# Attention in one Trainium2 core: written orders for VectorE and ScalarE, finer steps, other places of loads and another handover

## The chip, the cores and the metric

The kernel runs on one core of a Trainium2 chip. It has five engines that each work through their own list of instructions in order: TensorE (PE; its weight loads are listed apart as PEld), VectorE (DVE), ScalarE (ACT), GpSimd (POOL) and SyncE (SP), which here only issues DMAs. Sixteen DMA engines move the data. The metric is the device time of one execution in microseconds, as the median of the runs; a difference of 0.3% (4.4 us) is about what a measurement of this kernel can tell from no change.

## The reference, cut to what matters

One encoder layer over 1024 frames of width 1024, in float32:

```
h  = RMSNorm(x);  P = h @ W_in            # q, k, v of 8 + 8 heads of 64, forget values, gates
A  = causal softmax(q k^T / 8 + c[t] - c[s]) v        # 8 "fox" heads; c = running sum of log f
B  = softmax(q k^T / 8 + rel_bias[clip(t - s)]) v     # 8 "band" heads; own and 8 earlier chunks of 64
y  = sigmoid(gA) * (A @ Wa) + sigmoid(gB) * (B @ Wb)
x  = x + y @ W_out
x  = x + relu(RMSNorm(x) @ W_up)^2 @ W_down;  final RMSNorm
```

Every softmax is exact: the row's largest value is taken off before the exponential, and the sum divides the result at the end.

## The kernel before, in words

Every large product runs as three matmuls on values that are split in a high and a low part (`wh`, `wl` of a weight, `xh`, `xl` of an operand), and the projections use Strassen's seven products. The program has these stages: projections of q, k, v and gates (to about 412 us of the profile), **attention** (to about 687 us), the second branch product, whose tiles are called `m` (to 740 us), the output projection `o` (to 844 us), and the feed-forward part. Only attention and the branch product are touched by the change.

**A head of attention.** The 16 heads are worked through in the order of `HEADS`: heads 0 to 7 are fox heads (causal, widths of 128 to 1024 keys), heads 8 to 15 are band heads (at most 640 keys). A head has eight query blocks of 128 rows. For each block, *S* (`score`) makes the scores on PE in a PSUM tile `s`; the pool `pss` holds two of them. Then DVE adds the mask (`wide`) or the bias tile (`bc`) in place and takes the row's smallest value into `mn` (line 498, profiled as CUSTOM_DVE_ANT_0 with a short READ_ACCUMULATOR behind it; scores are negated, so the smallest is the largest). Then ACT takes the exponential into the probabilities `p` (line 509), and the `s` tile is free again. Then, for a group of up to four 128x128 blocks, *T* (`turn`) transposes `p` on PE into a PSUM tile `pt`, ACT rounds it to the high part `th` (line 829) and DVE takes the low part `tl` (line 830). *P* (`weigh`) multiplies `th` and `tl` with the values and sums in the one PSUM tile `pv`, which ACT copies to `both` (line 790). In the string of a head, the scores are those of the head after it.

**What sets the order.** On PE the order is written out: `FOX_TURN` and `BAND_TURN` are strings of letters S, T, P and F that are worked through once for each head, and everything on PE is issued through an object that keeps the program's order. `INTRO` brings a few letters forward. The DMAs on SP keep the program's order as well. On DVE, ACT and POOL the order is left to the scheduler, which places instructions by its own estimate of time; what comes out is a fixed list too, since each engine works through its list in order.

**Filling.** From head 9 on, the letter F puts three matmuls of the first branch product (`m_c_h_1`, 128 columns of gate and 512 frames each) between the attention's matmuls. Its weight `wrab` is loaded one block ahead (`fetch` in `fill`), rounded on ACT (line 718) and its low part made on POOL (line 720); the gate `z` is loaded too, and the result goes to `m_dram`.

**Loads of a head.** At the end of a head's scores, `load_head` issues `qk` and `sk` of the head after next and `load_bias` its bias tile (one DMA of 128x640, a negation on POOL on line 458, and two memsets that block the corners). After the second group of an odd head, `reciprocals` turns the sums of the exponentials into factors, writes them to `r_dram` in four DMAs and reads them back spread over partitions (`rb`, two DMAs) at once; POOL multiplies with them (line 811).

**Handover.** After the last head, the band heads' results are read back from `o_dram` (`olt`) and split for the branch product; then for each of 16 tiles the gate, the earlier part `m` and the product are put together, and split on POOL (lines 875 to 886).

Of the kernel before, what the change touches and what calls it, by code (L numbers as in the profile page):

```python
# [40 lines left out]
INTRO = "TTPTTTPP"  # L41
FOX_TURN = "TTTSPSTTPSPTTSPPTSTPTSPSPPPS"
BAND_TURN = "TSTFSFFTFPSTSTFPPSTFTSPPTSFFPSPP"
# [47 lines left out]
def hybrid_block(ctx: ExitStack, tc: tile.TileContext, xT, xN, g1, wall, wf, fb, relb, g2, g3, outT):  # L91
# [359 lines left out]
    def load_bias(n, eng):  # L451

        pr, hh = HEADS[n]
        if pr >= 4:
            return
        bc = biases[n] = aps.tile([P, BAND], F32, tag=f"bc{n % 2}", name=f"bc{n}")
        eng.dma_start(bc, relb[2 * pr + hh])
        G.tensor_scalar(bc, bc, -1.0, None, op0=ALU.mult)
        G.memset(bc[0:64, BAND - 64:BAND], BIG)
        G.memset(bc[64:128, 0:64], BIG)  # L460

    def load_head(n, eng):
# [4 lines left out]
        if n < 2:  # L467
            sks.append(p.tile([SK, 2, S], F32R, tag="sk", name=f"sk{n}"))
            G.memset(sks[n][HD:SK].bitcast(F32), 0.0)
            G.memset(sks[n][HD:HD + 3, 1, :].bitcast(F32), 1.0)  # L470
# [11 lines left out]
    def score(n, i, bank, te, ve):  # L482
# [5 lines left out]
        if i == 0:  # L488
            smalls[n] = aps.tile([P, 8], F32, tag=f"mn{n % 2}", name=f"mn{n}")
        spans = [(max(off, HALF * x), min(off + W, HALF * (x + 1))) for x in range(2 if off + W > HALF else 1)]  # L490
        rows = slice(i * P, (i + 1) * P)
        for t, w in enumerate((qk, sk)):
            for a, b in spans:
                keys = slice(j0 * P + a - off, j0 * P + b - off)
                te.matmul(bank[:, a:b], w[:, 1, rows], w[:, 0, keys], start=t == 0, stop=t == 1)
        x = bank[:, off:off + W]
        more = wide[:, S - W:S] if pr >= 4 else biases[n][:, BAND - W:BAND]
        ve.tensor_tensor_reduce(x, x, more, 1.0, 3.0e38, ALU.add, ALU.min, smalls[n][:, i:i + 1])  # L498

    def soften(n, i, bank):  # L500
# [7 lines left out]
        with tc.issue_after(sigmoids[-1]):  # L508
            A.activation(p[:, :W], bank[:, off:off + W], AF.Exp, scale=-1.0, bias=smalls[n][:, i:i + 1],  # L509
# [64 lines left out]
    def project_qk(pr):  # L574
        def out(row, h, src):
            t = etile("qk")
            V.scalar_tensor_tensor(t, src, -0.125 if row == 0 else 1.0, rstd[:, hs(h)], op0=ALU.mult, op1=ALU.mult)
# [53 lines left out]
    G.affine_select(out=wide[:, S - P:S], in_=wide[:, S - P:S], compare_op=ALU.is_ge, fill=BIG, base=0, pattern=[[-1, P]],  # L631
# [15 lines left out]
    sent = 0  # L647

    def send(te=TO):
        nonlocal sent  # L650
        if sent == len(chunks):
            return
        n, i = chunks[sent]
        bank = pss.tile([P, S], F32, tag="s", name="s")
        score(n, i, bank, te, V)
        soften(n, i, bank)
        sent += 1
        if i == 7 and n + 2 < 16:
            load_head(n + 2, LO)
            load_bias(n + 2, LO)  # L660

    for n, ins in enumerate(chain(steps, last)):
# [3 lines left out]
        with tc.issue_after(ins):  # L666
            for _ in range(AHEAD[n]):
                send()
# [7 lines left out]
    ol = opool.tile([P, 4, S], F32R, tag="ol", name="ol")  # L676
    apq.append(pool(astack, "apq1", "right"))
# [552 lines left out]
```

## Time and profile before

| | |
|---|---|
| median of 3 runs | 1457.67 us (1457.08 to 1460.63) |
| the profiled execution | 1460.32 us, of which 1458.6 us are the span of the instructions |
| PE, DVE, ACT, POOL busy | 96%, 59%, 48%, 59% of the span |
| mean granted TensorE clock | 0.991 |

A matmul's end is modelled in the profile and matmuls overlap, so a busy PE is not a PE at its best: what counts is how far one start is from the next. The sharpest reading is therefore by stages, in stretches that are cut where each head does the same thing.

### The profile page before, as it was taken

How to read it: one execution, taken by the hardware profiler on the slowest of the kernel's cores; microseconds unless marked ns; L12 is line 12 of the kernel's file. 1: busy time of each engine (PE TensorE's matmuls, PEld its weight loads, DVE VectorE, ACT ScalarE, POOL GpSimd, SP SyncE). 2: the span in 40 equal slices, each digit the busy share in tenths (PEclk: the TensorE clock that was granted, in tenths of full speed). 3: DMA queues.
4: the chain of work that ended last, by engine and by line, in shares of the span. 5: the costliest groups of instructions: out<-in, count | busy, mean ns of one | idle time of the engine just before them, and what ended most of it. 6: DMA issues, size and time to landing. Idle time of an engine off the chain costs nothing.

```text
span 1458.6 us, 20521 instructions
## 1 busy us (share of the span) xinstructions
PE 1402.2 (96%) x6658; PEld 1167.7 (80%) x6658; DVE 860.2 (59%) x1349; ACT 697.8 (48%) x1351; POOL 861.2 (59%) x688
## 2 busy tenths in 40 slices
PE   7999999999999988988999999999999999999997
PEld 5787888888878877877788888888888888888886
DVE  7756445443268865754428864444545568999644
ACT  8534333344358875655336543333333344344654
POOL 1377776778822253323783677777776645557463
PEclk9999999999999999999999999999999999999998
DMA  8546667763457688886756244444444875679263
GB/s 275 151 113 190 184 193 218 207 196 123 142 170 214 179 227 225 253 237 197 257 179 200 89 143 150 145 153 152 153 152 157 284 234 170 168 244 230 88 211 121
DMA packets 138069, 268.94 MB, mean 184 GB/s; under 512 B 19490, under 2 KB 21538, under 8 KB 134890
## 3 DMA queue, kind: packets, MB, share of 16 engines
q1 hardware_dynamic: 90106, 182.50, 41.1%
q10 hardware_dynamic: 44656, 77.26, 16.6%
q0 software_dynamic: 3200, 7.88, 2.4%
q8 instruction: 52, 0.85, 0.2%
q14 instruction: 55, 0.45, 0.1%
HBM read 173.49 MB, written 86.21 MB: 178 GB/s over the span
## 4 chain that ended last, share of the span: by engine, by line
PE 75%; DMA 7%; issue 5%; POOL 4%; DVE 4%; ACT 3%; SPq 0%; POOLq 0%; ACTq 0%; DVEq 0%
PE u L214 39%; PE dS L214 11%; PE dA L214 5%; PE o L214 5%; PE s L104 3%; PE pv L104 3%; PE m L214 3%; PE pt L104 3%; DMA wrab<-wall 2%; POOL wl_A L163 2%; DMA bc<-relb 2%; DMA wr<-wall 2%; PE m L104 1%; ACT p L509 1%; PE u L104 1%
## 5 line engine op out<-in xcount | busy, mean ns | idle before, releaser
L163 POOL TENSOR_TENSOR wl_A<-wr,wh_A 128x512 fp32r<-128x512 f32 x118 | 158.8, 1354 | 90.6 <-ACT wh_A L161 74.8
L163 POOL TENSOR_TENSOR wl_S<-S,wh_S 128x512 fp32r<-128x512 f32 x102 | 136.1, 1338 | 32.7 <-ACT wh_S L161 32.0
L161 ACT CAST wh_S<-S 128x512 fp32r<-128x512 f32 x105 | 64.6, 621 | 113.0 <-PE u L214 44.2
L830 DVE TENSOR_TENSOR tl<-pt,th 128x512 fp32r<-128x512 f32 (+1 forms) x144 | 89.7, 642 | 40.4 <-ACT th L829 39.8
L161 ACT CAST wh_A<-wr 128x512 fp32r<-128x512 f32 x105 | 64.9, 620 | 89.4 <-PE u L214 45.0
L509 ACT ACTIVATE p<-s,mn 128x640 f32<-128x640 f32 (+7 forms) x128 | 90.6, 710 | 34.1 <-DVE mn L498 32.6
L163 POOL TENSOR_TENSOR wl_S<-ks,wh_S 128x512 fp32r<-128x512 f32 x48 | 67.0, 1421 | 53.6 <-ACT wh_S L104 53.6
L567 DVE TENSOR_TENSOR u<-u,u 128x512 f32<-128x512 f32 x70 | 48.8, 697 | 74.4 <-PE u L214 71.7
L829 ACT CAST th<-pt 128x512 fp32r<-128x512 f32 (+1 forms) x144 | 76.6, 555 | 25.6 <-PE pt L104 25.0
L104 PE MATMUL pt<-ident,p 128*128 128x128 f32 x528 | 78.5, 279 | 7.9 <-DVE tl L830 7.7
L184 POOL TENSOR_TENSOR S<-wr,wr 128x512 f32<-128x512 f32 x35 | 46.0, 1314 | 57.4 <-DMA wr<-wall 37.0
L104 PEld LDWEIGHTS pt<-ident,p 128*128 128x128 f32 x528 | 63.6, 143 | 17.2 <-DVE tl L830 6.3
L104 PE MATMUL s<-qk 128*128 128x384 f32 (+2 forms) x192 | 59.6, 365 | 13.7 <-ACT p L509 13.7
L104 PE MATMUL pv<-th,v 128*128 128x512 f32 (+1 forms) x192 | 65.0, 348 | 4.2 <-ACT lo L787 2.1
L163 POOL TENSOR_TENSOR wl_A<-ka,wh_A 128x512 fp32r<-128x512 f32 x32 | 46.0, 1448 | 35.4 <-ACT wh_A L104 35.4
L104 PE MATMUL pv<-tl,v 128*128 128x512 f32 (+1 forms) x192 | 62.4, 344 | 2.2 <-DVE tl L830 2.2
L810 POOL TENSOR_TENSOR on<-on,lo 128x512 f32<-128x512 f32 x16 | 20.5, 1284 | 73.7 <-PE pv L104 40.7
L276 ACT CAST qkh<-qk 128x512 fp32r<-128x512 f32 x32 | 19.9, 621 | 88.3 <-DMA qk_dram<-qkl 34.0
L985 ACT ACTIVATE v<-v 128x512 f32<-128x512 f32 x64 | 40.3, 632 | 44.7 <-DVE v L984 44.7
L560 DVE TENSOR_TENSOR u<-u,c 128x512 f32<-128x512 f32 x35 | 24.5, 699 | 58.6 <-PE u L214 56.6
L498 DVE CUSTOM_DVE_ANT_0 s<-s,wide 128x128 f32<-128x128 f32 (+3 forms) x64 | 48.6, 764 | 14.0 <-PE s L104 13.5
L498 DVE CUSTOM_DVE_ANT_0 s<-s,bc 128x640 f32<-128x640 f32 (+2 forms) x64 | 42.4, 662 | 23.7 <-PE s L104 18.5
(420 smaller groups left out, 4705.2 us busy)
## 6 DMA issues: line engine op xcount, KB each, us to landing
wr<-wall SPq DMA_DIRECT2D x235, 256.0 KB, 3.6
a_dram<-at ACTq DMA_DIRECT2D x64, 256.0 KB, 2.7
xT<-a_dram SPq DMA_DIRECT2D x64, 256.0 KB, 4.7
qk<-qk_dram SPq DMA_DIRECT2D x15, 1024.0 KB, 8.7
qk_dram<-qkh ACTq DMA_DIRECT2D x96, 128.0 KB, 2.5
a_dram<-v ACTq DMA_DIRECT2D x48, 256.0 KB, 2.0
xB<-a_dram SPq DMA_DIRECT2D x44, 256.0 KB, 4.6
z_dram<-zt ACTq DMA_DIRECT2D x32, 256.0 KB, 2.2
```

The lines of the kernel that those rows point to most:

```text
L104: return lambda *a, **kw: tc.keep_in_program_order(getattr(self.eng, name)(*a, **kw))
L161: (act.tensor_copy if act is G else act.copy)(wh, src)
L163: lows.append(eng.tensor_tensor(wl, src, wh.bitcast(F32), op=ALU.subtract))
L184: eng.tensor_tensor(t, raw(3), raw(2), op=ALU.add)
L214: done = eng.matmul(bank, w[wi], x[xi], start=(first and t == 0), stop=(t == n - 1 and not part), skip_group_check=part or not first)
L498: ve.tensor_tensor_reduce(x, x, more, 1.0, 3.0e38, ALU.add, ALU.min, smalls[n][:, i:i + 1])
L509: A.activation(p[:, :W], bank[:, off:off + W], AF.Exp, scale=-1.0, bias=smalls[n][:, i:i + 1], accum_out=smalls["den", pr][:, 8 * hh + i:8 ...
L560: V.tensor_tensor(banks[1], banks[3], c22, op=ALU.add)
L567: V.tensor_tensor(banks[b], banks[b], u2, op=ALU.add)
L829: A.copy(th, pt)
L830: V.tensor_tensor(tl, pt, th.bitcast(F32), op=ALU.subtract)
L985: A.activation(v, v, AF.Square)
```

## The change

All attention steps get letters of their own, and DVE and ACT keep the program's order too: S makes the scores, R takes the smallest (DVE), E the exponential (ACT), T transposes, H rounds (ACT), L takes the low part (DVE), P multiplies, V copies `pv` out (ACT), F fills, M ends a filled tile (DVE), O splits a band head's result for the handover. There are strings for a fox head, a band head and the last head.

The scores are no longer negated: the mask and the bias tile carry minus the large number, and the smallest of the negated sum is taken in the same instruction by its factor of -1. So the bias tile is used as it is loaded: two tiles are kept, their corners are set once, and two DMAs of 64x576 fill the rest; the negation and the memsets of each head are gone. The bias is loaded when the smallest value of the last block has been taken, no longer with the scores. `rb` is read back when the head's `pv` has been copied out, no longer right after the write. Weights and gates for filling are fetched four tiles ahead instead of one, and their rounding stands in ACT's order.

At the end, the last head's results stay on the chip (`o3h`, `o3l`, made by DVE and ACT), the other band heads' results are read back and split while the last head runs (O), and the branch product begins with four tiles whose last quarter waits for the last head (`begun`). Its tiles come in another order, and the split behind it moves from POOL to DVE.

```diff
-INTRO = "TTPTTTPP"
-FOX_TURN = "TTTSPSTTPSPTTSPPTSTPTSPSPPPS"
-BAND_TURN = "TSTFSFFTFPSTSTFPPSTFTSPPTSFFPSPP"
+INTRO = "THLPTHLTTHPHLL"
+FOX_HEAD = "THSSRRETTSLPHEHTLSRTLPHERPHTSLTELSHVTPHRLRELTHSEPTSHLRPEPPLPHRLEPV"
+BAND_HEAD = "FFTSFHTHFRLSLRMPETSHETPLFRHETSPLRHFVSTPEHLTRHPLLSFETFPRHLESPPSMRRVEE"
+LAST_HEAD = "THLTHLFFFFMTHPPFLFFFMTPTHFLHFTFFPVLTMHPFHLTHFFFLPLOOOPOOMOPV"
...
     def load_bias(n, eng):
...
-        bc = biases[n] = aps.tile([P, BAND], F32, tag=f"bc{n % 2}", name=f"bc{n}")
-        eng.dma_start(bc, relb[2 * pr + hh])
-        G.tensor_scalar(bc, bc, -1.0, None, op0=ALU.mult)
-        G.memset(bc[0:64, BAND - 64:BAND], BIG)
-        G.memset(bc[64:128, 0:64], BIG)
+        if n < 10:
+            bands.append(aps.tile([P, BAND], F32, tag=f"bc{n % 2}", name=f"bc{n}"))
+            G.memset(bands[-1][0:64, BAND - 64:BAND], -BIG)
+            G.memset(bands[-1][64:128, 0:64], -BIG)
+        bc = biases[n] = bands[n % 2]
+        eng.dma_start(bc[0:64, 0:BAND - 64], relb[2 * pr + hh, 0:64, 0:BAND - 64])
+        eng.dma_start(bc[64:P, 64:BAND], relb[2 * pr + hh, 64:P, 64:BAND])
...
-        ve.tensor_tensor_reduce(x, x, more, 1.0, 3.0e38, ALU.add, ALU.min, smalls[n][:, i:i + 1])
+        ve.tensor_tensor_reduce(x, x, more, -1.0, 3.0e38, ALU.add, ALU.min, smalls[n][:, i:i + 1])
...
+    def take_lowest(ve=VO):
+        if len(cut) < len(chunks):
+            n, i = chunks[len(cut)]
+            lowest(n, i, made[len(cut)], ve)
+            cut.append(None)
+            if i == 7 and n + 2 < 16:
+                load_bias(n + 2, LO)
...
+        for _ in range(4):
+            fetch()
+        yield
+        halves(0)
         yield
         for n, (c, h) in enumerate(todo):
-            if n + 1 < len(todo):
-                fetch()
+            fetch()
+            if h == 0:
+                halves(c + 1)
...
+    def spread_reciprocals(pr):
         rb = ap0.tile([P, S], F32, tag="rb", name=f"rb{pr}")
...
+        if pr == 3:
+            VO.tensor_tensor(o, o, rb, op=ALU.mult)
+            AO.copy(o3h[:, hs(h)], o)
+            VO.tensor_tensor(o3l[:, hs(h)], o, o3h[:, hs(h)].bitcast(F32), op=ALU.subtract)
+            return
...
+    def round_p():
+        pt, th, tl = turns[0][len(turns[1])]
+        turns[1].append(AO.copy(th, pt))
+
+    def low_p():
+        pt, th, tl = turns[0][len(turns[2])]
+        turns[2].append(VO.tensor_tensor(tl, pt, th.bitcast(F32), op=ALU.subtract))
...
+    for c in range(4):
+        begun[c, 0] = psm[0].tile([P, HALF], F32, tag="d", name=f"m{c}_0_0")
+        branch(begun[c, 0], c, 0, range(3))
+    for c, h in [(c, h) for d in (0, 4) for h in range(2) for c in range(d, d + 4)]:
...
-        split((mop[h][0][:, c, :], mop[h][1][:, c, :]), m, G)
+        split((mop[h][0][:, c, :], mop[h][1][:, c, :]), m, V)
```

How the lists of the engines change at three places follows. In a row, `out<-in` are the program's names, with a number for each buffer.

**PE, end of one fox head and start of the next, before.** The row `s_4878` holds the last and widest scores (1024 keys) of the head after; `s_4915` the first ones of the head after that.

```order
L104 MATMUL pv_4786<-th_4832,v3_4477 128x256
L104 MATMUL pv_4786<-tl_4833,v3_4477 128x256
L104 MATMUL s_4878<-qk4_4495 128x512 x2
L104 MATMUL s_4878<-sk0_3800 128x512 x2
L104 MATMUL pt_4890<-ident_66,p4_0_4717 128x128
L104 MATMUL pt_4890<-ident_66,p4_1_4726 128x128
L104 MATMUL pt_4890<-ident_66,p4_2_4754 128x128
L104 MATMUL pt_4890<-ident_66,p4_3_4784 128x128
L104 MATMUL pt_4899<-ident_66,p4_1_4726 128x128
L104 MATMUL pt_4899<-ident_66,p4_2_4754 128x128
```

The same place in the changed kernel, where `s_4843` holds the widest scores:

```order
L105 MATMUL s_4843<-qk4_4457 128x512 x2
L105 MATMUL s_4843<-sk0_3800 128x512 x2
L105 MATMUL pv_4802<-th_4763,v3_4484 128x512
L105 MATMUL pv_4802<-tl_4764,v3_4484 128x512
L105 MATMUL pv_4802<-th_4776,v3_4484 128x512
L105 MATMUL pv_4802<-tl_4777,v3_4484 128x512
L105 MATMUL pv_4802<-th_4796,v3_4484 128x512
L105 MATMUL pv_4802<-tl_4797,v3_4484 128x512
L105 MATMUL pv_4802<-th_4822,v3_4484 128x384
L105 MATMUL pv_4802<-tl_4823,v3_4484 128x384
```

Before, the ten transposes of the next head follow the widest scores; now the last five P of the running head do, and one T of the next head after them.

**SP, end of a fox head that ends a pair, before.** `r_dram<-rt` writes the factors, `rb` reads them back, `qk`, `sk` and `bc` are the loads of the first band head.

```order
L104 DMA r_dram<-rt_5181 16x32 x4
L104 DMA rb_5189<-r_dram 64x1024 x2
L104 DMA on_1_5057<-both_1_5255 64x512
L104 DMA lo_1_5058<-both_1_5255 64x512
L104 DMA v_5259<-v_dram 128x1024
L104 DMA qk_5277<-qk_dram 128x2048
L104 DMA sk_3800<-sk_dram 64x2048
L104 DMA bc_5281<-relb 128x640
```

And now:

```order
L105 DMA r_dram<-rt_5197 16x32 x4
L105 DMA qk_5239<-qk_dram 128x2048
L105 DMA sk_3800<-sk_dram 64x2048
L105 DMA bc_5261<-relb 64x576 x2
L105 DMA v_5271<-v_dram 128x1024
L105 DMA on_1_5071<-both_1_5273 64x512
L105 DMA lo_1_5072<-both_1_5273 64x512
L105 DMA rb_5279<-r_dram 64x1024 x2
```

The read of `rb` has moved from behind its write to behind the head's copies, and the loads of the next heads stand ahead of it.

**ACT, start of a band head with filling, before**: the row `wh_ab` rounds the weight of the second filled block, and the exponentials `p` and roundings `th` of attention stand around it.

```order
L509 ACTIVATE p_3_5946,den_5883<-s,mn_5879 128x512
L790 COPY both_0_5975<-pv 128x512
L718 CAST wh_ab_5959<-wrab_5957 128x512
L829 CAST th<-pt 128x512
L509 ACTIVATE p_4_5986,den_5883<-s,mn_5879 128x640
```

The same block's rounding now:

```order
L105 ACTIVATE p_6_5869,den_5497<-s,mn_5720 128x640
L105 ACTIVATE p_7_5871,den_5497<-s,mn_5720 128x640
L105 CAST wh_ab_5877<-wrab_5540 128x512
L105 CAST th<-pt 128x512 x2
L105 ACTIVATE p_0_5927,den_5926<-s,mn_5913 128x128
```

The rounding stands half a head earlier, and its load `wrab_5540` is issued two heads ahead of it on SP, together with that of the first block.

More of the change, by code (lines that the diff above doesn't have):

```diff
@@ L630, in hybrid_block @@
     G.memset(wide, 0.0)
[L631 removed]
+    G.affine_select(out=wide[:, S - P:S], in_=wide[:, S - P:S], compare_op=ALU.is_ge, fill=-BIG, base=0, pattern=[[-1, P]],
                     channel_multiplier=1)
@@ L676, in hybrid_block @@
     ol = opool.tile([P, 4, S], F32R, tag="ol", name="ol")
+    o3h, o3l = [opool.tile([P, S], F32R, tag=t, name=t) for t in ("o3h", "o3l")]
     apq.append(pool(astack, "apq1", "right"))
@@ L839, in weigh_next @@
         weigh_at += 1
-        if js == order[0] and h and hh:
+        if weigh_at == len(groups) - 2:
+            normalise(pr, 0)
+        if js == order[0] and hh and h == int(n < 15):
             reciprocals(pr)
-        if js == order[-1]:
-            flush()
-            if h and n + 2 < 16:
-                load_values(n + 2)
-            if h and hh:
-                for x in range(2):
-                    normalise(pr, x)
-    acts = {"S": send, "T": turn, "P": weigh_next}
-    send()
@@ L852, in hybrid_block @@
-    turns = [t for n, (pr, hh) in enumerate(HEADS) for t in
-             (FOX_TURN if pr >= 4 else BAND_TURN if n >= FILL_FROM else BAND_TURN.replace("F", ""))]
-    for t in INTRO:
-        if t != "S":
-            turns.remove(t)
-    for n, t in enumerate(chain(INTRO, turns)):
-        if t == "F":
-            next(fills, 0)
-        else:
-            acts[t]()
-        if t == "S" and sent == 8 * FILL_FROM:
+        if js == order[-1] and h and n + 2 < 16:
+            load_values(n + 2)
@@ new lines, in done @@
+    def done(n, h):
+        pr, hh = HEADS[n]
+        flush()
+        if n == 15:
+            if h == 0:
+                spread_reciprocals(pr)
+            else:
+                normalise(pr, h)
+        elif h and hh:
+            for x in range(2):
+                o = outs[pr, x]
+                G.tensor_tensor(o, o, lows_o[pr, x], op=ALU.add)
+            spread_reciprocals(pr)
+            for x in range(2):
+                normalise(pr, x)
+    bands_o = [(j, h) for h in range(2) for j in range(3)]
@@ new lines, in hybrid_block, with filler, split_o @@
+    waiting = []
+    def filler():
+        nonlocal fill_at
+        next(fills, 0)
+        fill_at += 1
+        if fill_at in (56, 64):
+            for j, h in bands_o[fill_at // 64 * 3:fill_at // 64 * 3 + 3]:
+                waiting.append(tmp("olt"))
+                LO.dma_start(waiting[-1], o_dram[j, :, hs(h)])
+    def split_o():
+        j, h = bands_o.pop(0)
+        t = waiting[5 - len(bands_o)]
+        AO.copy(oh[:, j, hs(h)], t)
+        VO.tensor_tensor(ol[:, j, hs(h)], t, oh[:, j, hs(h)].bitcast(F32), op=ALU.subtract)
@@ L863, in hybrid_block @@
+    for t in chain(INTRO, heads):
+        acts[t]()
+        if t == "S" and len(made) in (8 * FILL_FROM - 4, 8 * FILL_FROM):
             next(fills)
-    for _ in fills:
-        pass
     flush()
```

164 lines of the change are left out of this document (94 added, 70 removed).

## The prediction

> **What bounds the kernel now.** The page first: PE is busy nearly all the time and no other engine comes near it.
>
> ```profile
> span 1458.6 us, 20521 instructions
> PE 1402.2 (96%) x6658; PEld 1167.7 (80%) x6658; DVE 860.2 (59%) x1349; ACT 697.8 (48%) x1351; POOL 861.2 (59%) x688
> ```
>
> That leaves 56 us of idle PE, and only what lies in the stretch that the change touches can be won. Next comes the table by windows, cut at the second exponential of each head (the starts of ACT L509 with 128x256): the first row holds six fox heads, then a row for each of the heads 7 to 14 (name them by the scores they hold, so the row from 513.09 makes the first band head's scores), then the last head, the handover, and the branch product.
>
> ```profile
> core 0: us, PE busy (x) PEld busy (x) DVE busy (x) ACT busy (x) POOL busy (x), PEclk, DMA share, GB/s
> 427.97:513.09 85.12, 79.77 (x500) 69.31 (x501) 69.21 (x163) 69.99 (x167) 19.03 (x17) 1.00 0.68 183
> 513.09:530.29 17.20, 13.62 (x85) 11.87 (x84) 11.91 (x30) 11.94 (x30) 11.54 (x12) 0.93 1.03 275
> 530.29:545.33 15.04, 14.02 (x78) 12.53 (x78) 9.81 (x25) 11.02 (x27) 4.88 (x6) 0.85 0.67 163
> 545.33:559.31 13.98, 12.46 (x84) 11.05 (x83) 10.09 (x28) 10.53 (x27) 9.27 (x10) 1.00 1.06 297
> 559.31:581.90 22.59, 17.71 (x103) 15.69 (x102) 11.53 (x27) 11.14 (x27) 5.88 (x6) 0.92 0.72 193
> 581.90:599.45 17.55, 17.35 (x108) 14.86 (x107) 12.12 (x30) 11.15 (x28) 5.89 (x6) 1.00 0.97 289
> 599.45:615.81 16.36, 16.36 (x105) 14.50 (x104) 11.41 (x27) 11.16 (x28) 4.69 (x5) 1.00 0.75 208
> 615.81:639.52 23.71, 17.41 (x100) 15.63 (x99) 11.74 (x29) 11.23 (x27) 7.09 (x7) 0.86 0.93 267
> 639.52:656.38 16.86, 16.86 (x106) 15.11 (x105) 11.50 (x27) 11.27 (x27) 4.65 (x5) 1.00 0.72 206
> 656.38:686.62 30.24, 26.59 (x161) 22.67 (x160) 16.74 (x33) 16.63 (x36) 10.02 (x8) 1.00 0.59 179
> 686.62:697.20 10.58, 7.23 (x31) 4.98 (x30) 3.48 (x4) 5.61 (x10) 7.54 (x7) 1.00 0.98 333
> 697.20:740.00 42.80, 42.80 (x189) 35.43 (x190) 14.10 (x19) 12.54 (x21) 33.28 (x27) 1.00 0.66 219
> ```
>
> Read the first number after the window (its length) against the next (PE busy). Heads with the same matmuls (100 to 108) take 16.36, 16.86 and 17.55 us, but also 22.59 and 23.71: the long ones have 4.9 and 6.3 us of idle PE and a granted clock of 0.92 and 0.86. The branch product (last row) has no idle PE, so nothing is to be won behind 697 us.
>
> The chain that ended last names what is late in the long rows.
>
> ```profile
> 514.29 11.79 DMA bc<-relb
> 526.16 1.84 POOL bc L458
> 559.08 11.75 DMA wrab<-wall
> 615.11 11.86 DMA bc<-relb
> 687.15 6.53 DMA olt<-o_dram
> 695.37 1.78 DVE ol L277
> ```
>
> Three loads of almost 12 us, two of a bias and one of a fill weight, stand in the first band head and in the two long ones; the handover waits for the results read back and their split.
>
> **The fox heads.** A row of six heads in 85.12 us is 14.19 us a head. What PE must do in it follows from two rows of the chain.
>
> ```profile
> 440.93 0.87 PE pt L104 x8
> 852.17 285.64 PE u L214 x1260
> ```
>
> A matmul of 512 columns costs 0.227 us when nothing waits (285.64/1260), a transpose 0.109. A fox head has 36 transposes (3.92 us) and 18432 columns of scores and values (36 x 0.227 = 8.16): 12.1 us. So 2.1 us a head are lost, the most that orders could win. The timeline shows two thirds of it at the head's end.
>
> ```profile
> 451.72 1.23 DVE L498 CUSTOM_DVE_ANT_0 s<-s,wide 128x1024 f32<-128x1024 f32 x1 [1.09 <-PE s L104]
> 452.79 0.50 PE L104 MATMUL pv<-th,v 128*128 128x512 f32 x1
> 452.87 0.69 DVE L830 TENSOR_TENSOR tl<-pt,th 128x512 fp32r<-128x512 f32 x1
> 453.36 1.16 ACT L509 ACTIVATE p<-s,mn 128x1024 f32<-128x1024 f32 x1
> 453.61 0.50 PE L104 MATMUL pv<-tl,v 128*128 128x512 f32 x1 [0.32 <-DVE tl L830]
> 454.66 0.39 PE L104 MATMUL s<-qk 128*128 128x256 f32 x1 [0.55 <-ACT p L509]
> ```
>
> `pv<-th` starts at 452.79 and streams 0.227, but `pv<-tl` starts at 453.61: 0.59 lost, because `tl` stood on DVE behind the widest smallest-value step (R). From 453.61 the next could start at 453.84, but S starts at 454.66: 0.82 lost until the widest exponential (E) frees its score tile. Together 1.41 a head.
>
> In the new order the `tl` of a group stands ahead of the widest R, and five P (4608 columns, 2.04 us) and a T (0.44) follow the widest S on PE. Count from that S: it ends at 0.91; R begins at 1.25, behind `tl`; E begins 1.33 after R's start (1.23 and the short read), at 2.6; the tile is free 1.30 after E's start (454.66 less 453.36), at 3.9. PE has work until 0.91 + 2.04 + 0.44 + 0.23 (first S of the next head) = 3.6. So 0.3 remains of 0.82, and the 0.59 goes. New is that the first narrow E stands on ACT behind E (to 3.7), the copy V and a rounding H (about 0.5 each): it ends near 5.2, while PE runs out at 4.8, so 0.4 comes back at the third S. Net 1.41 - 0.3 - 0.4 = 0.7 a head. **Term A**: 7 fox heads x 0.7 = -4.9; between 0 and -9.9 (7 x 1.41).
>
> **The loads.** SP shows why the first band head's bias is late.
>
> ```profile
> 501.76 1.97 SPq L104 DMA_DIRECT2D r_dram<-rt  x4
> 510.24 1.11 SPq L104 DMA_DIRECT2D rb<-r_dram  x2
> 513.30 0.43 SPq L104 DMA_DIRECT2D qk<-qk_dram  x1
> 514.29 1.40 SPq L104 DMA_DIRECT2D bc<-relb  x1
> ```
>
> `rb` holds SP from 503.7 to 510.2, since it reads what `r_dram` writes; `qk` and `bc` queue behind it, and then comes POOL's negation (1.84). Now `rb` stands behind the loads of the next heads, and the negation is gone: the bias is ready at least 1.8 us and up to 8 us earlier (6.5 + 1.8). It is used a whole head (13 to 16 us) after its issue, which covers 12 us. The eight DMAs more (two for one, a row of 2304 instead of 2560 bytes) cost SP about 0.5 us each and move no more bytes.
>
> **Term B**, first band head: 17.20 to a plain head's 14.2 = -3.0 (0 to -3.6, its idle PE). **Term C**, the two heads after it: 15% of 15.04 us of clock were lost behind that stall, -2.2 (0 to -4.7 with their idle PE of 1.02 and 1.52). **Term D**, 22.59: the wait was for `wrab`, issued less than a head ahead; it now is issued a head or two ahead of its rounding, so 11.75 us are covered by 16. To the mean of the undisturbed heads (16.36 and 16.86, so 16.6): -6.0. **Term E**, 17.55 and 23.71, the latter the bias again: -0.9 and -7.1. If the cover were too short in one of them, the stall would be back in full: 0 for D and E is the other bound, -15.6 the far one (all heads at 16.4).
>
> **The handover.** Last head and handover have 3.65 + 3.35 = 7.0 us of idle PE. Now the read back (6.53) runs under the last head and PE starts with three quarters of four tiles (36 matmuls, 8.2 us), under which the last copy, product and split run (six steps of 0.5 to 0.7 us, about 4). What is left: the splits O are on DVE.
>
> ```profile
> L277 DVE TENSOR_TENSOR ol<-olt,oh 128x512 fp32r<-128x512 f32 x7 | 7.6, 1123 | 3.9 <-ACT oh L276 3.9
> L277 POOL TENSOR_TENSOR ml<-m,mh 128x512 fp32r<-128x512 f32 x9 | 11.6, 1293 | 0.7 <-ACT mh L276 0.7
> ```
>
> At 1.12 us each against 0.68 of PE for a quarter, two of them cost 0.9; the last `tl` stands behind the wait for `rb`, say 0.6. **Term F**: -7.0 + 1.5 = -5.5 (0 to -7.0). The 16 splits that move from POOL to DVE cost 18 us there (16 x 1.12) in a stretch where DVE has 14.1, less the 7.6 that leave: 24.5 of 42.8, hidden under PE; without that cover the last one alone would cost 1.1. POOL loses 16 x 1.29 = 20.6. The Trainium skill (SBUF — State Buffer, "Who interferes with whom") says that a DVE instruction with two SBUF inputs and a GpSimd one that reads SBUF lock each other out for a whole instruction. The 1123 of these rows, against 640 for `tl`, agrees; by the rule each could take 0.64 + 1.29, together 31 us, and DVE would have 37 of 42.8: nothing by the sum, 1.9 instead of 1.1 for the last.
>
> **Term G**, what the closer packing costs. Over the five heads from 559.31 to 656.38, DMA share times length sums to 79.7 us, 15.9 a head, and heads are to take 16.6: 96% of what sixteen engines can do. Some loads will be late. I take +3.0 (0 to +12, the bias of D and E half kept and a stall as in the row 559.31 once).
>
> **Sum.** -4.9 - 3.0 - 2.2 - 6.0 - 8.0 - 5.5 + 3.0 = -26.6 us. Against its own time: 1460.32 (the span and 1.7 around it) - 26.6 = 1433.7. That execution was 2.65 above the median of 1457.67; the sum's parts do not depend on that, so the median goes to **1431**.
>
> **The rivals.**
>
> *DMA is the clock of the band heads.* For it: the 15.9 us above, shares of 0.93 to 1.06 in three rows, loads of 12 us. Against it: the head of 599.45 and the one of 639.52 ran at 0.75 and 0.72 without a stall. Then D and E stay (14.0), A to C and F come, and nothing more is lost: -26.6 + 14.0 - 3.0 = -15.6, so 1442.
>
> *The two score tiles bind the fox heads, whatever the order.* The two waits come back in each head with the same 0.3 and 0.55. The Trainium skill (Perfetto Trace Analysis, "Optimization Strategy") reads the same gap repeating on the engine that should be saturated as a sign of too little SBUF or PSUM for the next tile. By that an order wins nothing there, and A is 0: -21.7, so 1436. Against it, from rows alone: of the 1.41, 0.59 is a wait for `tl`, which no score tile causes.
>
> *It does not reach PE.* The orders of DVE and ACT were fixed lists before, too, and the loads may only be late elsewhere: the stall of 615.81 could fall on `v` or `qk`, which now follow each other in one burst. Then gains and new stalls cancel: within 4.4 us of 1457.7.
>
> *Slower: ACT in written order waits for a weight.* All exponentials stand behind the rounding `wh_ab`. If its load were late in each of the eight filled blocks, every microsecond would be PE's. It decides from 26.6/8 = 3.3 us each; at the 5 us seen once it gives 1431 + 40 = 1471. Against it: the load now has a head or two of lead.
>
> **How the numbers follow.** Chances: the forecast 0.58, DMA as the clock 0.19, the score tiles 0.14, no gain 0.05, slower 0.04. Faster by over 0.3% (4.4 us, what a measurement can tell): 0.58 + 0.19 + 0.14 = 0.91; same 0.05; slower 0.04. The forecast's own range is 1421 to 1440. All near bounds together (-9.9, -3.6, -4.7, -15.6, -7.0, no G) give -40.8, 1417; the DMA case reaches 1442 and, with G's upper bound half drawn, 1447. So 1418 to 1447.
>
> **What would show it.** In the profile after: fox heads 13.3 to 13.6 us apart (A); no wait for `bc` over 1 us and the first band head under 15 us (B, C); five filled heads of 16 to 17.5 us each, with a clock of 1.00 (D, E); from the last head's last P to the first branch matmul under 2 us of idle PE (F). It would be wrong if a load still stands in the chain with 10 us or more in the band heads, if DMA share there is at 1 with PE waiting, or if ACT waits for `wrab`.

## The result and the profile after

| | before | changed |
|---|---|---|
| median | 1459.15 us | 1440.45 us (1437.30 to 1441.12) |
| ratio | | 0.9863, 95% interval 0.9834 to 0.9892 |
| profiled execution | 1460.32 us | 1437.30 us |

The change makes the kernel 1.4% faster, 18.7 us by the medians. The forecast was 1431, with a range of 1418 to 1447. The two profiled executions are 23.0 us apart, more than the medians, since the changed kernel's is the fastest of its four.

The page of the changed kernel:

```profile
span 1435.6 us, 20509 instructions
PE 1398.8 (97%) x6658; PEld 1167.0 (81%) x6658; DVE 872.1 (61%) x1369; ACT 698.1 (49%) x1349; POOL 825.9 (58%) x650
```

The windows of the changed kernel, cut as before at the second exponential of a head (heads 2 to 7 in the first two rows, the first band head's scores in the second as well, then the heads 9 to 15 by the scores they hold, the last head, the handover, the branch product):

```profile
core 0: us, PE busy (x) PEld busy (x) DVE busy (x) ACT busy (x) POOL busy (x), PEclk, DMA share, GB/s
428.91:442.82 13.91, 13.66 (x76) 11.98 (x77) 9.98 (x23) 11.23 (x27) 0.00 (x0) 0.88 0.37 109
442.82:522.34 79.52, 78.57 (x506) 69.89 (x506) 69.41 (x166) 70.33 (x170) 23.81 (x22) 1.00 0.81 227
522.34:536.99 14.65, 13.84 (x90) 11.87 (x90) 11.81 (x31) 11.99 (x31) 6.84 (x7) 1.00 0.98 276
536.99:555.22 18.23, 15.09 (x90) 13.29 (x89) 11.06 (x25) 11.27 (x29) 8.66 (x9) 0.93 1.03 280
555.22:572.11 16.89, 16.89 (x105) 15.09 (x104) 11.57 (x29) 11.45 (x28) 2.57 (x2) 0.98 0.59 187
572.11:588.46 16.35, 16.35 (x104) 14.62 (x103) 11.51 (x27) 11.51 (x29) 5.11 (x4) 1.00 0.94 259
588.46:604.80 16.34, 16.34 (x104) 14.62 (x103) 11.76 (x30) 11.50 (x28) 1.73 (x2) 1.00 0.93 275
604.80:621.15 16.35, 16.35 (x105) 14.63 (x103) 11.51 (x27) 11.51 (x28) 5.87 (x5) 1.00 0.96 271
621.15:637.91 16.76, 16.64 (x104) 14.69 (x103) 11.67 (x30) 11.40 (x28) 1.02 (x1) 1.00 1.00 296
637.91:665.34 27.43, 27.43 (x161) 23.93 (x160) 16.89 (x35) 15.53 (x34) 12.88 (x11) 1.00 0.77 240
665.34:673.00 7.66, 4.30 (x20) 3.23 (x19) 5.65 (x7) 6.46 (x12) 4.14 (x3) 0.93 0.91 324
673.00:716.54 43.54, 43.54 (x187) 35.53 (x187) 25.80 (x34) 15.30 (x25) 28.03 (x20) 0.97 0.67 212
```

Fox heads are 13.25 us apart (79.52/6), all filled heads 16.3 to 16.9; the heads of 22.59 and 23.71 us are gone. Three rows are bad: 13.91 at a clock of 0.88, 18.23 with 3.1 us of idle PE, and 7.66 with 3.4.

What PE waited for, from 420 us to the end of the branch product (total, times, longest), in the kernel before:

```profile
PE s L104 <- ACT p L509: 13.7, 13, 6.3
PE pt L104 <- DVE tl L830: 7.7, 3, 4.9
PE pv L104 <- DVE tl L830: 2.2, 7, 0.3
```

and in the changed one:

```profile
PE pv L105 <- ACT th L105: 3.1, 1, 3.1
PE s L105 <- DVE tl L105: 2.1, 1, 2.1
PE m L105 <- POOL oh L860: 1.9, 1, 1.9
PE s L105 <- ACT p L105: 1.8, 8, 0.7
PE pv L105 <- DVE tl L105: 1.3, 5, 0.3
```

The waits of the three kinds in the first list go from 23.6 us (two long ones of 6.3 and 4.9 among them) to 3.1, the last two rows of the second. Those that head the second list happen once each, at three places: the start, the handover and the first filled tile.

The gain by stage follows, as time lost: how far the starts of successive matmuls lie apart beyond their streaming (0.227 us for 512 columns, 0.109 for a transpose). It counts a low clock too, and doesn't depend on where a cut falls in the program. The seven heads lie between the second exponentials of head 8 and head 15.

| us lost in | start | fox heads | seven heads | last head to branch product | sum |
|---|---|---|---|---|---|
| before | 3.1 | 16.2 | 23.8 | 9.5 | 52.6 |
| changed | 5.9 | 7.8 | 10.2 | 6.5 | 30.5 |
| `old_fox` | 6.3 | 13.5 | 18.4 | 7.0 | 45.2 |
| `rb_at_write` | 6.8 | 15.2 | 24.7 | 6.9 | 53.7 |
| `rb_both3` | 6.8 | 10.8 | 20.4 | 6.0 | 44.0 |
| `both3` | 6.8 | 6.4 | 17.5 | 6.6 | 37.4 |
| `bias_old` | 6.6 | 6.4 | 12.9 | 6.0 | 31.9 |
| `fetch_early` | 6.7 | 6.3 | 14.5 | 6.4 | 33.9 |
| `first_fill` | 6.7 | 6.4 | 13.8 | 7.6 | 34.6 |
| `intro` | 3.7 | 7.7 | 11.2 | 6.6 | 29.2 |
| `handover` | 5.9 | 7.9 | 14.3 | 2.7 | 30.7 |
| `load_more` | 6.8 | 6.5 | 24.2 | 6.9 | 44.4 |
| `best` | 2.7 | 6.5 | 10.6 | 0.7 | 20.5 |
| `best_less` | 2.6 | 6.4 | 4.6 | 0.7 | 14.4 |

The rows below the second are the experiments. The changed kernel, `intro` and `handover` have the same program in the seven heads, and lose 10.2, 11.2 and 14.3 us there: a difference of 4 us in that column alone says nothing.

### The profile page after: what moved, and what is told of

It is laid out like the page before. It is cut to its first block, busy times and chain, and to the rows that moved or that the text cites. A ratio compares the mean times of both kernels' runs of the same rounds, so it can differ in the third digit from the quotient of the medians.

```text
span 1435.6 us, 20509 instructions
## 1 busy us (share of the span) xinstructions
PE 1398.8 (97%) x6658; PEld 1167.0 (81%) x6658; DVE 872.1 (61%) x1369; ACT 698.1 (49%) x1349; POOL 825.9 (58%) x650
## 4 chain that ended last, share of the span: by engine, by line
PE 84%; DVE 4%; issue 3%; DMA 3%; POOL 2%; ACT 2%; SPq 1%; POOLq 0%; ACTq 0%; DVEq 0%
PE u L215 42%; PE dS L215 12%; PE dA L215 8%; PE o L215 5%; PE s L105 4%; PE m L215 3%; PE pt L105 3%; PE pv L105 3%; PE m L105 2%; PE u L105 1%; DMA wr<-wall 1%; DMA lo<-both 1%; DMA rb<-r_dram 1%; DVE s L105 1%; ACT th L105 1%
## 5 line engine op out<-in xcount | busy, mean ns | idle before, releaser
L164 POOL TENSOR_TENSOR wl_S<-S,wh_S 128x512 fp32r<-128x512 f32 x102 | 136.2, 1338 | 30.9 <-ACT wh_S L162 30.3
L105 ACT ACTIVATE p<-s,mn 128x640 f32<-128x640 f32 (+4 forms) x121 | 85.9, 710 | 14.9 <-DVE mn L105 13.2
L105 PE MATMUL pv<-th,v 128*128 128x512 f32 (+3 forms) x180 | 61.8, 353 | 3.1 <-ACT th L105 3.1
L571 DVE TENSOR_TENSOR u<-u,c 128x512 f32<-128x512 f32 x35 | 24.5, 699 | 57.5 <-PE u L215 55.4
L105 PE MATMUL pv<-tl,v 128*128 128x512 f32 (+3 forms) x180 | 57.7, 339 | 1.3 <-DVE tl L105 1.3
L105 DVE CUSTOM_DVE_ANT_0 s<-s,bc 128x640 f32<-128x640 f32 (+2 forms) x64 | 42.3, 661 | 24.7 <-PE s L105 17.6
L1072 DVE SCALAR_TENSOR_TENSOR v<-u,rstd 128x512 f32<-128x512 f32 x64 | 43.9, 688 | 20.1 <-PE u L215 18.1
```

The lines of the kernel that those rows point to most:

```text
L105: return lambda *a, **kw: tc.keep_in_program_order(getattr(self.eng, name)(*a, **kw))
L164: lows.append(eng.tensor_tensor(wl, src, wh.bitcast(F32), op=ALU.subtract))
L571: V.tensor_tensor(banks[1], banks[3], c22, op=ALU.add)
L1072: V.scalar_tensor_tensor(v, src, 0.0, rstd[:, hs(h)], op0=ALU.max, op1=ALU.mult)
```

## The experiments

All are edits of the changed kernel. Ratios are against the kernel before, run on the same chip.

**The fox heads' order undone (`old_fox`).**

```diff
-             (FOX_HEAD if pr >= 4 else ...
+             (OLD_FOX if 0 < n < 8 else ...
+              "RE" + BAND_HEAD ...
+OLD_FOX = "THTHTHRELSRELPLSRTTHLEHPSRPVELTTSRHHLLEPPTSRHLTHELPTSRHLEPSRPPPVES"
```

> The changed kernel, but the eight strings of the fox heads have PE, VectorE and ScalarE in the order in which the kernel before had them (the widest smallest-value step and its exponential stand behind the scores that end a head, the low part behind them). Theory (term A): the order alone makes a fox head 13.27 us instead of 14.22, so the heads come out 14.0 to 14.3 us apart here, and the time is 6 to 7 us above the changed kernel's (1440), about 1447. Rival: the fox heads gained from something else (no negation, loads moved away), so the old order in the new kernel gives about 13.3 us a head and 1440.

Measured: 1452.56 us, ratio 0.9961 (0.9943 to 0.9980). The window of the heads 3 to 8:

```profile
443.41:529.32 85.91, 80.71 (x506) 69.70 (x505) 70.02 (x165) 71.43 (x169) 28.15 (x26) 1.00 0.76 206
```

The widest smallest-value step and its exponential (R, E) now stand in the string of the next head. 14.32 us a head against 13.25, with the same loads and the same bias: the order alone is worth 1.07 us a head. The time rose by 12 us, not by 7; the rest is in the band heads (18.4 lost against 10.2), where PE in this execution also waited 3.8 us for `qk` and `sk`. That part wasn't expected, and what delays those loads was not followed further.

**The bias as before (`bias_old`).**

```diff
         if i == 7 and n + 2 < 16:
             load_head(n + 2, LO)
+            load_bias(n + 2, LO)
...
+        eng.dma_start(bc, relb[2 * pr + hh])
+        G.tensor_scalar(bc, bc, 1.0, None, op0=ALU.mult)
...
-            if i == 7 and n + 2 < 16:
-                load_bias(n + 2, LO)
```

> The changed kernel, but the bias is loaded as before: one load of 128x640 with the head's scores, a pass of POOL over the tile (it multiplies by 1 here, in place of the negation) and two memsets, in each head. Theory 1 (the prediction's terms B and E charge the late bias to the queue behind the read back of the factors and to POOL together): with the read back moved, a load of 12 us and POOL's 1.8 us are still covered by a head of 13 to 16 us, so less than 1 us comes back, about 1440. Theory 2: the negation and the earlier issue were what made the bias late; then the first band head or two of the filled heads show a wait of 2 to 6 us for it, and the time is 3 to 10 us longer, 1443 to 1450.

Measured: 1443.01 us, ratio 0.9900 (0.9878 to 0.9922). POOL waits for the bias (up to 10.8 us at once), but VectorE and PE in no head. The interval overlaps with the changed kernel's: of the change's many edits this one is not where the gain lies.

**The factors read back at once (`rb_at_write`, `rb_both3`).**

```diff
             LO.dma_start(rows[b], rt[32 * b:32 * b + 16, :])
+        if pr != 3:
+            spread_reciprocals(pr)
...
-            spread_reciprocals(pr)
```

> The changed kernel, but the factors are read back right behind their write, as before, in all pairs but the last. Theory (the prediction's B and E): the read holds SP for some 6 us in every second head, and the loads behind it (scores' operands, bias, values) come late: waits of 2 to 6 us in the band heads, 3 to 10 us slower than the changed kernel although the wait at 548 us goes, so 1440 to 1448. Rival: with the bias used as loaded and weights fetched early nothing in that queue is urgent; the wait of 3.6 us at 548 us goes and 3 to 5 us are gained, about 1436.

Measured: 1457.87 us, ratio 1.0004 (0.9981 to 1.0027). This one call put back takes the whole gain, more than either theory said. What ScalarE waited for in this run (total, times, longest), and the longest of these waits in its timeline:

```profile
ACT both L105 <- DMA lo<-both: 23.9, 5, 10.1
```

```profile
553.57 0.19 ACT L105 ACTIVATION_READ_ACCUMULATOR p<-s,mn 128x1 f32 x1
563.83 0.59 ACT L105 COPY both<-pv 128x512 f32<-128x512 f32 x1 [10.07 <-DMA lo<-both]
564.31 0.80 ACT L105 ACTIVATE p<-s,mn 128x640 f32<-128x640 f32 x1
```

The copy `both` needs a buffer, both buffers wait for their stores `on` and `lo`, and these stand on SP behind the read that waits for its own write. In the written order the next exponentials stand behind the copy. So the order on ScalarE turns a late store into a stall of PE (8.6 us at 556 us). A third buffer should mend that:

```diff
-            both = ap0.tile([P, HALF], F32, tag="both", name=f"both{n}_{h}", bufs=2)
+            both = ap0.tile([P, HALF], F32, tag="both", name=f"both{n}_{h}", bufs=3)
```

> As the run with the factors read back right behind their write (1458, no gain over the kernel before), with three buffers for the copy of a head's result. Theory: the 17 us that the early read back costs come through these copies (ScalarE stood 23.9 us, five times, for one, with the exponentials behind it), so most of it comes back: 1440 to 1448. Rival: the loads of operands and bias behind the read back are late themselves, and the copies only show it first: 1452 or more, with waits for qk, sk or bc in the place of those for p.

Measured: 1456.84 us, ratio 0.9993 (0.9972 to 1.0013): almost nothing came back, and the theory falls. (The profiled execution, 1452.06 us, is the fastest of twelve, so its row in the table flatters it.) In this run ScalarE no longer waits for the stores of `both`, but for the fill weights, VectorE for the bias, and PE for operands and values (first row ScalarE, second VectorE, then PE):

```profile
ACT wh_ab L105 <- DMA wrab<-wall: 11.3, 4, 4.4
DVE s L105 <- DMA bc<-relb: 6.2, 2, 3.6
```

```profile
PE pv L105 <- ACT th L105: 9.4, 5, 3.3
PE s L105 <- ACT p L105: 2.7, 7, 1.0
PE s L105 <- DMA sk<-sk_dram: 2.7, 4, 0.9
PE pv L105 <- DMA v<-v_dram: 2.5, 3, 1.0
```

So several loads behind that read on SP are late, and which of them stops PE changed with one buffer more.

**A third buffer in the changed kernel (`both3`)**, the same edit alone:

> The changed kernel, but with three buffers instead of two for the copy of a head's result (both). Theory: what the changed kernel loses from one execution to the next (1437 to 1441, and waits of 1 to 2.7 us for p in the profiles of the last runs) are copies that wait on ScalarE for a buffer whose stores are still under way, with the next exponentials behind them in the written order; with a third buffer no wait of over 0.6 us for p is left in the band heads and the time is 1 to 4 us lower, about 1437. Rival: the third buffer only moves the wait to the next thing that the DMA queue makes late (operands, values, the factors): 1440.

Measured: 1440.89 us, ratio 0.9885 (0.9858 to 0.9911): no gain. No wait for `both` on a store is left, and the profiled execution lost 7.1 us at the first filled tile instead (3.6 in the changed kernel).

**The first fetches earlier (`fetch_early`).**

```diff
-        if t == "S" and len(made) in (8 * FILL_FROM - 4, 8 * FILL_FROM):
+        if t == "S" and len(made) in (8 * FILL_FROM - 24, 8 * FILL_FROM):
```

> The changed kernel, but the first four fetches for filling (two weights, four gates, 1.5 MB) are issued two and a half fox heads earlier, at 226 GB/s and a DMA share of 0.81, and not between the first two band heads, where the trace has 276 GB/s and a share of 0.98 to 1.03. Theory: DMA is the clock of just this passage (the two runs with a changed start, and the one with later filling, lost there what they gained elsewhere), so the read back of the factors lands early enough: the 3.6 us wait at 548 us shrinks to under 1, no wait of 1.5 us behind a copy of the result, clock 1.00: 3 to 6 us faster than the changed kernel, about 1436. Rival: the read back is late because it stands behind its neighbours in SP's order, whatever they load: the wait keeps over 2.5 us and the time is 1440.

Measured: 1443.75 us, ratio 0.9907 (0.9884 to 0.9929). The wait at the first filled tile stays, 3.8 us in this run:

```profile
PE m L105 <- POOL oh L860: 2.5, 1, 2.5
...
PE m L105 <- POOL ol L861: 1.3, 1, 1.3
```

So the volume of these fetches is not what makes the factors late. The rival holds: `rb` stands behind `qk`, `sk`, `bc` and `v` on SP.

**The first filled tile later (`first_fill`).**

```diff
+FIRST_FILL = "FFTSFHTHRLSLRPETSHETPLFRHETSMPLRHFFVSTPEHLTRHPLLSFETFPRHLESPPSMRRVEE"
-             (... BAND_HEAD if n >= FILL_FROM else
+             (... FIRST_FILL if n == FILL_FROM else BAND_HEAD if n > FILL_FROM else
```

> The changed kernel, but in the first head with filling the fourth matmul group of the first filled tile, which is the first to need the last fox pair's result, is issued about 3 us of PE work later. Theory: the 3.6 us that PE stands there at 548 us (POOL had to wait for the factors, whose read back now stands behind the next head's loads) go away, with the clock of 0.93 behind it: 3 to 5 us faster than the changed kernel, about 1436. Rival: the filling was covering other waits in this head, which now open instead: under 1.5 us gained.

Measured: 1440.95 us, ratio 0.9890 (0.9865 to 0.9915). At this place 1.2 us are lost and not 3.6, but new losses of 1.6, 2.4 and 0.8 us come up in later heads (ahead of each ScalarE stands at `both`, for 3.9, 4.7 and 3.1 us). No gain.

**The start (`intro`) and the handover (`handover`).**

```diff
-INTRO = "THLPTHLTTHPHLL"
+INTRO = "TTRHTHELPLPHTLHL"
...
     make_scores()
-    take_lowest()
-    take_exp()
...
-        heads.remove(t)
+        if t not in "RE":
+            heads.remove(t)
```

> The changed kernel, but ahead of the first head ScalarE rounds two groups of probabilities before it takes the widest exponential (in the changed kernel the exponential stands first and the rounding behind it), and PE turns two groups before it multiplies. Theory: the 3.2 us that PE waits for the first rounding at 420.8 us, and the granted clock of 0.88 in the 14 us behind it, are a cost of the written order; at most 1.5 of the 5.6 us lost between 420 and 429 us stay and the clock is 1.00 behind it: 3 to 5 us faster than the changed kernel, about 1436. Rival: the wait only moves to the second scores, which need the tile that the widest exponential frees: less than 1 us gained, 1440.

Measured: 1439.31 us, ratio 0.9879 (0.9855 to 0.9902). The start loses 3.7 instead of 5.9 us: 0.7 of the 3.2 at the first rounding are left, and 1.9 instead of 0.9 are lost at the third scores, which wait for the widest exponential's tile as the rival said. The granted clock in the head behind it (427.28 to 441.10 us) is 0.88 as in the changed kernel, and not the 1.00 that was expected. In the time it can't be told from the changed kernel.

```diff
-LAST_HEAD = "THLTHLFFFFMTHPPFLFFFMTPTHFLHFTFFPVLTMHPFHLTHFFFLPLOOOPOOMOPV"
+LAST_HEAD = "THLTHLFFFFMXXXXTHPPFLFFFMTPTHFLHFTFFPVWLTMHWPFHLTWHFFFLWPLOOOMNPPVOOO"
...
```

X loads a branch weight, W rounds it, and N makes the first half of the last result.

> The changed kernel, but in the last head the first four weights of the branch product are loaded and rounded earlier, in ScalarE's written order, so that the rounding of the last probabilities does not stand behind two casts that wait for them; the last low part and the first three splits stand on VectorE ahead of the work on the first half of the last result, which waits for the factors; three of the six splits come behind the last copy. Theory: the 4.7 us lost between 665 and 673 us go to under 1.5 and the clock behind it stays at 1.00 (0.97 over 43.5 us now, 1.2 us): 3 to 5 us faster than the changed kernel, about 1436. Rival: the results read back land at about 665 us whatever the order, so the wait moves to the first branch matmul: under 1.5 us gained.

Measured: 1439.48 us, ratio 0.9885 (0.9865 to 0.9906). The last stage loses 2.7 instead of 6.5 us, as the theory said, but this execution's seven heads lost 4 more. In the time it can't be told from the changed kernel either.

**More bytes (`load_more`).**

```diff
+    spare = cpool.tile([P, 6, P], F32, tag="spare", name="spare")
...
+            if i % 4 == 3 and 9 <= n < 15:
+                LO.dma_start(spare, v_dram[n % 8, i // 4, :, 0:6])
```

> The changed kernel, with two loads of 384 KB more in each of the heads 9 to 14, into a tile that nothing reads (0.77 MB on top of some 4.5 MB a head). Theory 1 (the rival of the prediction, DMA as the clock of the band heads, now as a limit that is near): 5.3 MB at the 296 GB/s of the fullest head are 17.8 us against 16.35, so the filled heads become 17.5 to 19 us long and the time grows by 6 to 15 us, to about 1450. Theory 2: the share of 0.93 to 1.00 is packets that wait and not a full engine; the heads stay at 16.4 and the time within 2 us of 1440.

Measured: 1452.55 us, ratio 0.9974 (0.9958 to 0.9990), as theory 1 had it. The seven heads of the changed kernel and of this one, in one window each:

```profile
522.34:637.91 115.57, 111.50 (x690) 98.81 (x690) 80.90 (x195) 80.62 (x193) 31.80 (x28) 0.99 0.92 263
```

```profile
522.03:651.54 129.51, 117.42 (x690) 102.90 (x690) 81.71 (x195) 80.42 (x194) 31.38 (x28) 0.93 0.99 269
```

4.7 MB more (12 x 0.393) cost 13.9 us, 339 GB/s: nearly every byte costs time. By an estimate at 269 GB/s the changed kernel's 30.4 MB (115.57 x 263) need 113 us, 98% of what it takes; at the 296 GB/s of its own row from 621.15 they would need 103. So the stage is near the limit of DMA, but that limit is not one number. In the changed kernel it shows in the first two of the seven heads, at a share of 0.98 and 1.03; the five behind them have 0.1 us of idle PE.

**All mends (`best`)**: `intro` (with one low part less), `handover` (the last high part on VectorE), `first_fill`, `both3`, and the values loaded behind `rb` in the last fox head.

```diff
+INTRO = "TTRHTHELPLPHTLH"
...
-            AO.copy(o3h[:, hs(h)], o)
+            VO.tensor_copy(o3h[:, hs(h)], o)
...
-        if js == order[-1] and h and n + 2 < 16:
+        if js == order[-1] and h and n + 2 < 16 and n != 7:
             load_values(n + 2)
...
             spread_reciprocals(pr)
+            if n == 7:
+                load_values(9)
```

> The changed kernel with the changed start (and the fourth low part left behind the first smallest values), the changed handover (with the high part of the last result made on VectorE), the later fourth group in the first filled tile, three buffers for the copies, and the values of the head after next loaded behind the read back of the factors in the last fox head. Theory: the gains of the parts (2 to 3 us at the start, 4 to 5 at the handover, 3 to 5 in the first filled head) add up, since with three buffers late stores no longer stand in front of exponentials: 8 to 13 us under the changed kernel, 1428 to 1433. Rival: DMA in the first band heads takes back what the start and the first filled head gain, and only the handover stays: 1435 to 1437.

Measured: **1429.44 us** (1427.43 to 1432.60), ratio 0.9806 (0.9777 to 0.9834): faster than both kernels. The start and the end add up as expected (2.7 and 0.7 us lost), and the wait at the first filled tile is gone, but the seven heads take as long as in the changed kernel: the first two 27.8 us instead of 32.9, the five behind them 88.2 instead of 82.7. Their window, and what ScalarE now waits for:

```profile
517.24:633.23 115.99, 110.55 (x690) 97.70 (x690) 80.55 (x195) 80.85 (x194) 30.91 (x27) 1.00 0.97 261
```

```profile
ACT wh_ab L106 <- DMA wrab<-wall: 6.4, 4, 3.4
```

**Fewer bytes (`best_less`).**

```diff
-        loads.append(eng.dma_start(sk[0:HD].bitcast(F32), sk_dram[e]).ins)
+        if n < 10:
+            loads.append(eng.dma_start(sk[0:HD].bitcast(F32), sk_dram[e]).ins)
```

> As the version with all mends (1429), but the low parts of queries and keys (sk, 0.5 MB a head) are not loaded any more for the heads 10 to 15; these heads work with the low parts of older heads. This leaves out 3 MB of the 30.3 MB that the seven heads from the second exponential of head 8 to that of head 15 move in 116 us. Theory 1 (DMA is the clock of these heads: with all mends they took 116.0 us at a DMA share of 0.97, no less than the changed kernel's 115.6, and the wait only went from the factors to the fill weights): 3 MB at some 280 GB/s are 10.7 us, of which PE can use what it lost; the five filled heads come to 16.4 to 16.8 us, the seven to 109 to 112, and the time to 1422 to 1426. Theory 2 (the waits are a matter of order on SP and of buffers, not of volume): the seven heads stay at 115 to 117 us and the time within 2 us of 1429.

Measured: 1424.18 us (1421.37 to 1425.47), ratio 0.9779 (0.9752 to 0.9806). The seven heads:

```profile
517.12:627.07 109.95, 109.35 (x690) 97.47 (x690) 80.86 (x195) 80.90 (x194) 33.90 (x30) 1.00 0.88 255
```

This kernel leaves out 3.1 MB of loads (six of 512 KB). The seven heads take 6.0 us less, the five filled heads are at 16.2 to 16.9, and of the waits of PE, VectorE and ScalarE for loads one of 0.6 us is left. The window moved 28.0 MB instead of 30.3, since some of the loads behind it came into it. The step is small: the intervals of the two ratios overlap, though every execution of this kernel is faster than every one of `best`, and kernels that have these heads alike differ by 4 us there.

Together with `load_more` this says that the loads and stores bound the band heads once the other waits there are mended. It doesn't say whether the bytes do it or the places on SP: the added loads made SP wait 10.3 us for `spare` in these heads, and without `sk` the 13.2 us that SP waits for its landings in `best` go to 2.0. The DMA share, 0.97 in `best` and 0.88 here, speaks for the bytes.

## Why the prediction was right, and where it was not

The kernel became faster by more than a measurement can tell, and the time lies in the range, 9.4 us above 1431. Of these 3.6 are in the sum (-26.6 forecast, -23.0 between the profiled executions), 3.1 are what the profiled execution lies under the median after, and 2.7 what the forecast took off because the one before lay above its median. The two rivals without a gain, no effect on PE and slower, fall with that. By lost time the parts are -8.4 (A and B), -13.6 (C to E with G), -3.0 (F) and +2.8 (the start): the first two sums came out near their forecasts of -7.9 and -13.2; F and the start, which was in no term, did not. Of the signs named ahead, that of F looked at the wrong place: between the last P and the branch product PE has no idle time, but 2.7 us inside the last P steps. And one sign against the forecast came: in the row of 18.23 us the DMA share is 1.03 while PE stands for 3.1. The far bound of D and E is -15.1 by its rows (97.07 less 5 x 16.4) and not -15.6, on which nothing hangs.

- **A and B, the fox heads and the first band head**: -7.9 forecast, -8.4 lost time less. Each fox head gained 0.9 us (14.19 to 13.25) and not 0.7: nothing is left of the 0.3 at the widest exponential, and of the 0.4 at the third scores the row below shows 0.16 us of idle PE. The low clock behind the start takes 1.7 us of that back. `old_fox` shows that the order does it. The first band head went from 17.20 us to 13.27 (509.07 to 522.34), -3.9 and beyond B's bound of -3.6, which counted idle PE and left out that head's clock of 0.93. B charged its late bias to `rb` and the negation together. `bias_old` puts the negation back and VectorE doesn't wait, so the negation alone is not it. That the place of `rb` was it is read from SP in the trace before and not shown for this head: `rb_at_write` lost its time at `both`, and the two waits for the bias in `rb_both3` are in later heads.

```profile
455.76 0.44 PE L105 MATMUL s<-qk 128*128 128x384 f32 x1 [0.16 <-ACT p L105]
```

- **The rival of the two score tiles** falls: with the same two tiles, the repeated waits of 0.32 and 0.55 us have become one of 0.16. The Trainium skill (Perfetto Trace Analysis, "Optimization Strategy") says that such a repeated gap can mean a lack of buffers; here the order removed most of it.
- **D and E** are right: 22.59, 17.55 and 23.71 us became 16.89, 16.35 and 16.35, -14.3 against -14.0. The cover is not quite the one that was forecast: in the changed kernel the weights of the second and third filled block are issued some 20 us ahead of their rounding, those of the later ones only 6 to 12 us, and they landed in time. No run puts the fetches alone back to one tile ahead. With them four tiles ahead and `rb` back at its write the seven heads lose 24.7 us (`rb_at_write`), about as much as before, so the lead of the weights alone is not enough; whether it is needed was not shown.
- **C is wrong**: the two heads behind the first band head took 29.02 us and now 32.88, with 18 matmuls more (4.1 us), so nothing was gained. The step that moved `rb` behind the loads named only what was freed and not who waits for `rb`: POOL's products, and behind them the first filled tile, which now begins 22.9 us and not 26.7 behind head 8's second exponential. The chain of the changed kernel has it, step by step:

```profile
539.31 7.81 DMA rb<-r_dram
547.28 2.51 POOL on L855 x2
549.79 1.11 POOL oh L860 x2
550.90 1.23 POOL ol L861
```

- **G**, the allowance of 3 for loads that come late, is about what this wait took (3.6). C to E with G came to -13.6 against -13.2, and that is partly luck: G was meant for loads that the closer packing makes late, and what used it up was the place of `rb` on SP (`fetch_early`).
- **F, the handover**, is half of what was forecast: -3.0 against -5.5. The last low part was put at 0.6. The timeline of the changed kernel shows 2.4:

```profile
665.10 0.69 DVE L105 TENSOR_TENSOR on<-on,rb 128x512 f32<-128x512 f32 x1 [1.72 <-DMA rb<-r_dram]
665.46 1.31 ACT L162 CAST wh_ab<-wr 128x512 fp32r<-128x512 f32 x2 [2.80 <-DMA wr<-wall]
666.68 0.58 ACT L105 CAST th<-pt 128x512 fp32r<-128x512 f32 x1
667.16 0.62 ACT L105 CAST o3h<-on 128x512 fp32r<-128x512 f32 x1
667.81 1.40 DVE L105 TENSOR_TENSOR o3l<-on,o3h 128x512 fp32r<-128x512 f32 x1 [2.01 <-ACT o3h L105]
669.14 0.68 DVE L105 TENSOR_TENSOR tl<-pt,th 128x512 fp32r<-128x512 f32 x1
669.87 0.45 PE L105 MATMUL s<-tl,v 128*128 128x384 f32 x1 [2.11 <-DVE tl L105]
```

  `tl` stands on VectorE behind `o3l`, which needs ScalarE's `o3h`; this stands behind two casts of branch weights whose loads come late. The prediction saw the wait for `rb` on one engine, and not that two written lists hold each other up. `handover` takes that apart and gets its 3.8 us.
- **The start was not in the sum at all**: +2.8 us lost. In the changed kernel the widest exponential stands on ScalarE ahead of the first rounding:

```profile
421.05 1.22 DVE L105 CUSTOM_DVE_ANT_0 s<-s,wide 128x1024 f32<-128x1024 f32 x1
422.37 1.11 ACT L105 ACTIVATE p<-s,mn 128x1024 f32<-128x1024 f32 x1 [3.03 <-DVE mn L105]
423.47 0.58 ACT L105 CAST th<-pt 128x512 fp32r<-128x512 f32 x1
424.10 0.49 PE L105 MATMUL pv<-th,v 128*128 128x512 f32 x1 [3.07 <-ACT th L105]
```

  Before, the rounding came first, by the scheduler's choice. The mean granted clock was then 0.88 over 13.91 us, some 1.7 us more (0.12 x 13.91), which the table counts among the fox heads. The Trainium skill (TensorE: Matmul & The Clock Gate, Part 1) puts the array at half its clock after about 3.4 us without work. Here shorter waits stood ahead of it: this one is 3.07 us, and in `intro`, with the same 0.88 behind it, none is over 1.8.
- **DMA as the clock of the band heads** was given 0.19, with the price of D and E. Its reason is borne out (`load_more`, and less clearly `best_less`), its price was not: the 113 us that 30.4 MB need at 269 GB/s are what the forecast left for the seven heads (126.1 - 16.2 + 3.0 = 112.9). So D and E could come, and little beyond them: three mends at places where PE stood in these heads gave nothing there.
- **ScalarE waiting for a weight** exists (1.0 us once in the changed kernel, 6.4 in four waits in `best`, or 1.6 each), and not at 5 us in each block.
- **The splits that moved to VectorE** took 1.13 us each, as forecast, and VectorE was busy for 25.80 us of the branch product (forecast 24.5). No idle PE came of it: all 43.54 us of that row are busy.

## What to carry to other kernels

A fixed order on an engine ties everything behind an instruction to the buffer that this one needs: before writing one, list for each instruction whose store or load frees its output, and what stands ahead of that on the queue. A read that waits for its own write belongs behind the loads on a shared queue, but then name who waits for the read. When mends at several places change the names of the waits and not the length of a stage, add and take away bytes: two such runs pointed here at what the mends had not, though each also changes what the queue waits for.

## What was not expected of the hardware

With loads and stores mixed on one core, the sixteen DMA engines gave 269 GB/s at a share of 0.99 (`load_more`) and 261 at 0.97 (`best`) over seven heads, mostly in pieces of 128 KB to 1 MB; in single rows it was more, 296 at 1.00 in the changed kernel. The Trainium skill (DMA: Bandwidth & Descriptors, "Bandwidth") has 425 GB/s for a 16 MB load on 128 partitions and 358 for the memory's side; by an estimate from the lower of these 30.4 MB would take 85 us and DMA would bind nothing here. The measurement decides. Many of the transfers here (`sk`, `bc`, `rb`, `on`, `lo`) cover 64 partitions; whether that is the reason was not tried.

A stage in which PE, VectorE and ScalarE work through the same fixed lists still varied by 4 us (115.6, 116.6 and 119.6 us for the seven heads in three kernels that have them alike). Near the limit of DMA the landing of loads may decide that; that this is also why the changed kernel's four executions lie 3.8 us apart was not shown.
